# Two-layer GLA/NSA trunk with mixture of experts on one core: float32 diagonal products in the attention, three experts kept on chip for the combination, a tail that works on pairs of tiles, a branch hint for the TensorE

## The chip, the core and the metric

The kernel runs on one NeuronCore of one Trainium2 chip. Five engines work side by side, each with its own instruction stream in fixed order: PE (TensorE, matrix products), DVE (VectorE), ACT (ScalarE), POOL (GpSimd) and SP (SyncE, which here only issues DMAs). The metric is the device time of the core in microseconds (us), the median of several executions. The profile comes from one further execution, whose own time stands beside its span below.

## The reference, cut to what matters

The input x is 512 tokens by 1024 features in float32. Layer 0 is gated linear attention, layer 1 is native sparse attention (NSA), and each is followed by a mixture of 16 experts of which every token uses two. After each of the four parts the residual is added and a layer norm is taken.

```
for i in range(DEPTH):                       # 2 layers: GLA, then NSA
    h = mixer(x)
    x = layer_norm(DN_ALPHA * x + h, ln_g[i, 0], ln_b[i, 0])
    f = moe_ffn(x, ...)                      # 16 experts, top 2, SwiGLU
    x = layer_norm(DN_ALPHA * x + f, ln_g[i, 1], ln_b[i, 1])
```

In moe_ffn an expert computes silu(x Wg) * (x Wu), times the gate weight of the token, and then the down product with Wd; a token's result is the sum over its two experts. In NSA the selected-block and the window branch each are a masked softmax over causal keys followed by a product with the values V; with 512 tokens, 8 blocks of 64 and a window of 512 both cover all causal keys.

## The kernel before, in words

Tokens lie in four tiles t = 0..3 of 128. To keep float32 accuracy with fast products, most operands are split in two float16 parts (hi and lo), and a product is three float16 products: hi*hi, hi*lo, lo*hi. ACT makes hi, DVE or POOL makes lo as the difference.

**Experts (moe, L810 to L962).** Each expert takes up to CAP = 96 tokens. `collect` (L839) gathers the token rows of expert e by one-hot matrices `ohe` on PE, `hot` (L828) makes those matrices on POOL. The gate/up products stand in L910 to L912, the hidden part `hh` is evacuated by ACT and DVE, and the down product is L944 to L946. While expert e is computed, `dispatch(e + 2)` collects the one after next, and `take` splits weights on ACT (L179) and DVE (L181). Weights come by SP's DMAs into seven staging buffers. The result rows `y` of experts 0 to 13 go to a DRAM table `yslots` (L955), and when expert 13's rows have landed, POOL issues eight indirect DMAs (L959) that add the two rows of each token to x: the order of (choice c, tile t) is (0,0), (0,1), (1,0), (0,2), (1,1), (0,3), (1,2), (1,3), and the second of a tile waits for its first. The last KEEP = 2 experts stay on chip: their rows are kept as float16 pairs `yh` (L949, L950), and `add_last` (L352) multiplies them by transposed one-hot matrices `ohT` on PE (L359) and adds the result to x, either on DVE (L369) or by an ACT copy (L366) and a POOL add (L367).

**A branch.** `dense_moe` (L964) handles an expert with more than 96 tokens. Every engine loads the largest load `rt_ci` (L966) and branches (L967). For these inputs the branch body, some 865 instructions of PE, is jumped over in both layers. The branch stands in expert 0: in layer 0 PE meets it in the middle of its gate/up product, in layer 1 at the end of it.

**Attention of layer 1 (nsa_attn, L1375).** It handles units (t, g, b): token tile t, key group g, branch b. The eight units of t = 3 come first, then t = 2, 1, 0. A unit makes score tiles for key tiles j = t..0 (L1418, L1419), ACT takes exp into `pf` (L1421), POOL masks the diagonal tile j = t (L1424), and `split` makes hi (ACT L1386, L1388 or DVE L1390 by the table HI_BY) and lo (DVE L1394; off the diagonal two of three on POOL, L1392, by LO_BY). `pv` multiplies by V: three float16 products per head and key tile (L1435 to L1437). Scores run two units ahead. Output projections and norms of finished tiles are placed between the units (ATTN_FILL).

**Tail (finish_out, L320).** After layer 1's experts the sums of all four tiles are formed by add_last (OUT_ADD says which halves go by ACT and POOL), and tiles (0,1) and then (2,3) are normed: statistics, a chain of one-column operations for the inverse root of each tile (ln_scale, L307), two 512-wide passes for each half tile, on DVE or (four of eight) on ACT and POOL, and the store.

The instruction order is the scheduler's, close to the order of the code.

Of the kernel before, what the change touches and what calls it, by code (L numbers as in the profile page):

```python
# [9 lines left out]
F32 = mybir.dt.float32  # L10
F16 = mybir.dt.float16
BF16 = mybir.dt.bfloat16
I32 = mybir.dt.int32
# [20 lines left out]
LO_BY = 'pdp'  # L34
OUT_ADD = (0, 0), (1, 0), (1, 1), (1, 1)
OUT_DVE = 1, 5, 6, 7
OUT_DIR = -1
PRELUDE = ("r0 r1 o0 t2 r2 oa s2 ob rt rs c0 t3 s3 r3 c1 xb",
# [16 lines left out]
RINGS = "aaallll" * 3 + "aaalllll" * 3 + "aaa", "aaallll" * 7  # L55
KEEP = 2
HS = 16.0
NEG = -1e30


class Trunk:
# [258 lines left out]
    def finish_out(self, store):  # L320
        nc = self.nc
        V = nc.vector
        lng, lnb = self.moe_ln
        scales, after = {}, None
        for t in range(NT):
            self.add_last(t, OUT_ADD[t])
        for pair in ((0, 1), (2, 3)):
            for t in pair:
                for n in range(2):
                    with self.behind(after):  # L330
                        last = V.bn_stats(self.bns[t][:, n], self.x[t][:, n * 512:n * 512 + 512])
            for t in pair:
                with self.behind(last):
                    self.bn = self.bns[t]
                    _, mean, z, b = self.ln_scale()
                    after = V.scalar_tensor_tensor(b, mean, -1.0, z, op0=OP.mult, op1=OP.mult)
                scales[t] = mean, z, b
            for t in pair[::OUT_DIR]:
                mean, z, b = scales[t]
                for h in range(2):  # L340
                    hs = slice(h * 512, h * 512 + 512)
                    s, g, o = self.x[t][:, hs], lng[:, hs], lnb[:, hs]
                    if 2 * t + h in OUT_DVE:
                        V.scalar_tensor_tensor(s, s, mean, g, op0=OP.subtract, op1=OP.mult)
                        V.scalar_tensor_tensor(s, s, z, o, op0=OP.mult, op1=OP.add)
                    else:
                        nc.scalar.activation(s, s, AF.Identity, bias=b, scale=z)
                        nc.gpsimd.tensor_mul(s, s, g)  # L348
                        nc.gpsimd.tensor_add(s, s, o)  # L349
                    store(t, h)  # L350

    def add_last(self, t, pool=()):  # L352
# [457 lines left out]
    def moe(self, layer, xT, ahead=()):  # L810
# [89 lines left out]
        first = []  # L900
        for e in range(NE):
            wg, wu, wd = self.W[e]
            xh, oh = XH.pop(e)
# [18 lines left out]
            hh = self.tmp([P, 2, 2, CAP], F16, "hh", 2)  # L922
            h3 = h.rearrange("p (f c) -> p f c", f=2)
            hh_ins = self.hilo(hh[:, 0], hh[:, 1], h3)
            nc.scalar.activation(g[:CAP, 1:3], o, AF.Copy, scale=IWS / HS, accum_out=gs)
            if e == 0:
                self.dense_moe(layer, xT, gm, ci)
            if e + 2 >= AHEAD:
                dispatch(e + 2)
            self.take(2, () if e else (sg_ins,))  # L930
            self.take(1, () if e else (sg_ins,))
            if e == NE - 2:
                first = [self.load_unit(src, slot="l") for src in ahead]
                self.ring = False
            if e >= NE - KEEP:
# [20 lines left out]
            if e == NE - KEEP - 1:  # L956
                for c, t in ((0, 0), (0, 1), (1, 0), (0, 2), (1, 1), (0, 3), (1, 2), (1, 3)):
                    j = c * NT + t
                    nc.gpsimd.indirect_dma_start(  # L959
                        out=self.x[t], out_offset=None, in_=self.yslots[:],  # L960
                        in_offset=bass.IndirectOffsetOnAxis(ap=gi[:, j:j + 1], axis=0), compute_op=OP.add)
        return first  # L962

    def dense_moe(self, layer, xT, gm, ci):  # L964
        nc, tc, a = self.nc, self.tc, self.a
        load = nc.values_load(ci[0:1, 0:1], min_val=0, max_val=2 * S)  # L966
        with tc.If(load > CAP, preferred_fallthrough_block=False):  # L967
            dm = self.tmp([P, NT, NE], F32, "rt_dm", 1)
# [104 lines left out]
    def nsa_proj(self, first, PT):  # L1073
# [9 lines left out]
        kB = [PT([P, 4, S], f"kB{b}") for b in range(2)]  # L1083
        V = [[PT([P, 4, 129], f"V{b}{t}") for t in range(NT)] for b in range(2)]
        qA = [PT([P, NT, 4, P], f"qA{g}") for g in range(4)]
        qB = [PT([P, NT, S], f"qB{g}") for g in range(4)]
# [285 lines left out]
        rest = lambda: v1(0), lambda: v1(1), lambda: cv(0), lambda: cv(1)  # L1372
        return (kcA, kcB, vc, kA, kB, V, qA, qB, gate), rest

    def nsa_attn(self, T, pool, early, rest, kcA, kcB, vc, kA, kB, V, qA, qB, gate):  # L1375
        nc = self.nc
# [3 lines left out]

        def split(hi, lo, src, ps=None):
            i = cnt[0]
# [6 lines left out]
            else:  # L1389
                nc.vector.tensor_copy(hi, src)  # L1390
            if ps is not None and LO_BY[i % len(LO_BY)] == "p":
# [21 lines left out]
        def scores(t, g, b):  # L1413
            ph = self.wp.tile([P, 4, 2, S], F16, name="ph", tag="wst", bufs=NST)
            for j in range(t, -1, -1):
# [3 lines left out]
                nc.tensor.matmul(st, kB[b][:70, g, js], qb(g, t), start=False, stop=True)  # L1419
                pf = T([P, S], "pf", F32, 3)  # L1420
                self.exp_ins = nc.scalar.activation(pf, st, AF.Exp)  # L1421
                if j == t:
                    v = pf.rearrange("p (h q) -> p h q", h=4)
                    nc.gpsimd.affine_select(v, v, pattern=[[0, 4], [1, P]], compare_op=OP.is_ge, fill=0.0,  # L1424
                                            base=0, channel_multiplier=-1)
                split(ph[:, j, 0], ph[:, j, 1], pf, None if j == t else st)
            return ph

        def pv(t, g, b, ph):
            ob = self.bank()  # L1430
            for h in range(4):
                hs = slice(h * P, (h + 1) * P)
                o0 = ob[:, h * 65:(h + 1) * 65]
                for j in range(t + 1):
                    nc.tensor.matmul(o0, ph[:, j, 0, hs], V[b][j][:, g, 0:65], start=(j == 0), stop=False)  # L1435
                    nc.tensor.matmul(o0[:, :64], ph[:, j, 0, hs], V[b][j][:, g, 65:129], start=False, stop=False)
                    nc.tensor.matmul(o0, ph[:, j, 1, hs], V[b][j][:, g, 0:65], start=False, stop=(j == t))  # L1437
            return ob
# [206 lines left out]
```

## Time and profile before

| what | value |
|---|---|
| median of 3 runs | 992.65 us (988.48 to 994.8) |
| the profiled execution's own time | 996.98 us |
| its span (first to last instruction) | 995.3 us |
| PE busy | 868.1 us (87%) |
| DVE busy | 767.5 us (77%) |
| ACT busy | 571.5 us (57%) |
| POOL busy | 353.4 us (36%) |
| mean granted TensorE clock | 0.94 |

The span divides into stages with different limits: layer 0's attention to about 240 us, its experts to 411, the NSA projections to about 587, the attention units to 746, routing to about 795, layer 1's experts to 957, and the tail. A row of a timeline gives start, duration, engine, line, operation, result and operands, and in brackets how long the engine was idle before it and what ended the wait; "issue" is a wait for nothing that the profile shows.

### The profile page before, as it was taken

What the parts mean: (1) busy time and instruction counts of PE and PEld (TensorE: products, weight loads), DVE (VectorE), ACT (ScalarE), POOL (GpSimd) and SP (SyncE); (2) the same over time, 40 slices, a digit from 0 to 9 for tenths busy, and PEclk for the clock granted to TensorE, in tenths of its full rate; (3) what the DMA queues carried; (4) which work ended last, traced back from release to release, by engine and by line L of the source; (5) the groups of instructions that cost most, each with busy time, mean ns of one, the idle gap of its engine ahead of it and who ended that gap; (6) DMA issues with size and microseconds to landing.
All of it is one profiled execution on the core that took longest, in us unless ns stands there. A gap on an engine that the chain in (4) does not pass through costs nothing. (4 is left out here: it accounts for less than half of the span.)

```text
span 995.3 us, 26759 instructions
## 1 busy us (share of the span) xinstructions
PE 868.1 (87%) x11266; PEld 708.6 (71%) x11266; DVE 767.5 (77%) x1675; ACT 571.5 (57%) x1196; POOL 353.4 (36%) x375
## 2 busy tenths in 40 slices
PE   7999999995799999699989989787987569999960
PEld 2478888875788888488978868465766558988840
DVE  5962226989699998797697756898798969999738
ACT  4832432542499999515535347765447149999821
POOL 0210120023135330540384425686532319523056
PEclk9999999997799999999999999788999679999995
DMA  9652231253499995942330010300018349999282
GB/s 299 222 207 86 85 114 57 86 213 127 142 385 394 368 380 213 213 143 83 128 127 3 2 43 2 129 2 1 2 47 336 128 149 409 380 380 379 100 154 100
DMA packets 29393, 169.64 MB, mean 170 GB/s; under 512 B 3536, under 2 KB 4176, under 8 KB 12752
## 3 DMA queue, kind: packets, MB, share of 16 engines
q1 hardware_dynamic: 23168, 144.49, 38.7%
q0 software_dynamic: 2960, 12.32, 5.7%
q10 hardware_dynamic: 3136, 11.01, 3.0%
q8 instruction: 93, 1.52, 0.6%
q14 instruction: 36, 0.29, 0.1%
HBM read 153.91 MB, written 13.89 MB: 169 GB/s over the span
## 5 line engine op out<-in xcount | busy, mean ns | idle before, releaser
L828 POOL TENSOR_SCALAR ohe<-icap,rt_px 128x96 f16<-128x96 f32 x112 | 111.6, 1011 | 153.2 <-PE bank L915 144.5
L181 DVE SCALAR_TENSOR_TENSOR whl<-wsu,whl 128x512 f16<-128x512 f32 x192 | 127.3, 713 | 3.0 <-ACT whl L179 2.2
L181 DVE SCALAR_TENSOR_TENSOR whl<-wst,whl 128x512 f16<-128x512 f32 x116 | 75.5, 702 | 67.3 <-ACT whl L179 67.2
L839 PE MATMUL bank<-ohe,xs 128*128 128x96 f16 x2048 | 103.7, 215 | 15.6 <-issue 8.6
L839 PEld LDWEIGHTS <-xs 128*128 128x128 f16 x2048 | 98.7, 104 | 16.6 <-issue 12.1
L179 ACT ACTIVATE whl<-wsu 128x512 f16<-128x512 f32 x192 | 106.8, 624 | 3.3 <-PE bank L259 3.2
L179 ACT ACTIVATE whl<-wst 128x512 f16<-128x512 f32 x144 | 80.8, 624 | 29.9 <-PE bank L250 9.8
L181 DVE SCALAR_TENSOR_TENSOR wha<-wst,wha 128x512 f16<-128x512 f32 x144 | 93.9, 703 | 1.7 <-ACT wha L179 1.7
L257 PE MATMUL bank<-whl,xt 128*128 128x256 f16 x320 | 88.1, 275 | 0.8 <-ACT xt L232 0.7
L259 PE MATMUL bank<-whl,xt 128*128 128x256 f16 x320 | 87.4, 274 | 1.4 <-DVE xt L233 1.4
L258 PE MATMUL bank<-whl,xt 128*128 128x256 f16 x320 | 88.1, 275 | 0.0
L179 ACT ACTIVATE wha<-wst 128x512 f16<-128x512 f32 x144 | 79.7, 622 | 2.5 <-DMA wst<-moe 2.5
L910 PE MATMUL bank<-xh,whl 128*128 128x96 f16 x576 | 75.2, 206 | 0.0
L911 PE MATMUL bank<-xh,whl 128*128 128x96 f16 x576 | 75.2, 206 | 0.0
L912 PE MATMUL bank<-xh,whl 128*128 128x96 f16 x576 | 75.2, 206 | 0.0
L259 PE MATMUL bank<-whl,oT 128*128 128x256 f16 x256 | 70.6, 276 | 2.2 <-DVE oT L233 2.2
L257 PE MATMUL bank<-whl,oT 128*128 128x256 f16 x256 | 70.7, 277 | 0.8 <-ACT oT L232 0.5
L258 PE MATMUL bank<-whl,oT 128*128 128x256 f16 x256 | 70.6, 276 | 0.0
L258 PE MATMUL bank<-whl,xT 128*128 128x256 f16 x256 | 69.8, 273 | 0.0
L259 PE MATMUL bank<-whl,xT 128*128 128x256 f16 x256 | 69.8, 273 | 0.0
L257 PE MATMUL bank<-whl,xT 128*128 128x256 f16 x256 | 69.8, 273 | 0.0
L911 PE MATMUL bank<-xh,wha 128*128 128x96 f16 x448 | 62.7, 212 | 4.3 <-issue 4.3
(388 smaller groups left out, 2813.2 us busy)
## 6 DMA issues: line engine op xcount, KB each, us to landing
wsu<-moe SPq DMA_DIRECT2D x54, 1024.0 KB, 7.8
wst<-moe SPq DMA_DIRECT2D x42, 1024.0 KB, 7.9
wst<-gla_in SPq DMA_DIRECT2D x11, 1024.0 KB, 4.8
yslots<-y ACTq DMA_DIRECT2D x28, 384.0 KB, 6.9
wst<-nsa_in SPq DMA_DIRECT2D x9, 1024.0 KB, 4.8
wst<-gla_out SPq DMA_DIRECT2D x4, 1024.0 KB, 4.8
wha<-nsa_out SPq DMA_DIRECT2D x4, 1024.0 KB, 4.9
xs<-xT SPq DMA_DIRECT2D x4, 512.0 KB, 7.1
```

The lines of the kernel that those rows point to most:

```text
L179: self.hi_ins = nc.scalar.activation(hl[:, 0, s], st[:, s], AF.Copy, scale=WS)
L181: nc.vector.scalar_tensor_tensor(hl[:, 1, s], st[:, s], WS, hl[:, 0, s], op0=OP.mult, op1=OP.subtract)
L257: nc.tensor.matmul(out, xt[0][:, k], w[0][:, s], start=(k == 0), stop=False)
L258: nc.tensor.matmul(out, xt[0][:, k], w[1][:, s], start=False, stop=False)
L259: nc.tensor.matmul(out, xt[1][:, k], w[0][:, s], start=False, stop=(k == KT - 1))
L828: eng.tensor_scalar(part[e][0][:, t], self.icap, self.px[:, t, e:e + 1], None, op0=OP.is_equal)
L839: nc.tensor.matmul(banks[half][:, j * CAP:(j + 1) * CAP], xs[t][:, i, k * P:(k + 1) * P], oh[:, t], start=(j == 0 and t == self.order[0] a ...
L910: nc.tensor.matmul(o, w[0][:, s], xh[:, 0, k], start=(k == 0), stop=False)
L911: nc.tensor.matmul(o, w[1][:, s], xh[:, 0, k], start=False, stop=False)
L912: nc.tensor.matmul(o, w[0][:, s], xh[:, 1, k], start=False, stop=(k == KT - 1))
```

## The change

It has five parts. (1) Attention: for t = 0, 1, 2 the diagonal tile j = t is no longer split; exp writes it as float32, and PE multiplies it with a float32 copy `VF` of V in one float32 product per head. Six `VF` tiles are made by ACT when V is evacuated. For these t POOL makes no lo parts any more (`share` only for t = 3). (2) KEEP is 3: expert 13 stays on chip too, so the gathers follow expert 12, and the combination takes six products for each half tile instead of four. (3) Gate/up of expert 15 comes before the down product of 14. (4) The branch body follows the branch directly, and PE gets a prefetch hint that the branch is likely taken; one hint for each layer. (5) Tail: tiles 0 and 1 are summed on DVE; for tiles 2 and 3 PE adds x itself, by a float32 product with the identity, so that their statistics and their first pass read PSUM; the small operations run for two tiles at once on two columns; three half tiles go over ACT and POOL.

```diff
-KEEP = 2
+KEEP = 3
+HINT = mybir.BranchHintType.__args__[0]
@@ finish_out
-        for t in range(NT):
-            self.add_last(t, OUT_ADD[t])
+        for t in (0, 1):
+            self.add_last(t)
+            src[t] = [self.x[t][:, h * 512:h * 512 + 512] for h in range(2)]
+        for t in (2, 3):
+            src[t] = self.sum_last(t)
...
+            st = self.tmp([P, 6, 2], F32, "lnp", 2)
...
+            for c in (3.0, 12.0, 768.0):
+                V.tensor_mul(u, z, z)
+                V.tensor_mul(u, u, v)
+                V.scalar_tensor_tensor(z, u, c, z, op0=OP.subtract, op1=OP.mult)
+            after = V.scalar_tensor_tensor(b, mean, -1.0, z, op0=OP.mult, op1=OP.mult)
...
+    def sum_last(self, t):
...
+            self.nc.tensor.matmul(ps, self.identf, self.x[t][:, ns], start=True, stop=False)
+            for e in range(KEEP):
+                for i in range(2):
+                    self.nc.tensor.matmul(ps, self.ohT[:CAP, e, t * P:(t + 1) * P], self.yh[e][:CAP, i, ns],
+                                          start=False, stop=(e == KEEP - 1 and i == 1))
@@ moe
+        self.tc.mark_branch_hint_location(f"dense{layer}", HINT, [mybir.EngineType.PE])
...
+        for e in range(NE):
+            sg_ins = up(e)
+            if e == 0:
+                self.dense_moe(layer, xT, gm, ci)
+            if e + 2 >= AHEAD:
+                dispatch(e + 2)
+            self.take(3, () if e else (sg_ins,))
+            if e == NE - 2:
+                first = [self.load_unit(src, slot="l") for src in ahead]
+                self.ring = False
+                continue
+            if e == NE - 1:
+                down(NE - 2)
+            down(e)
@@ dense_moe
-        with tc.If(load > CAP, preferred_fallthrough_block=False):
+        with tc.If(load > CAP, label=f"dense{layer}"):
@@ evac_v
+                    if tp * 2 + j < NT - 1:
+                        vf = VF[b][tp * 2 + j]
+                        nc.scalar.activation(vf[:, :, 0:64], ps[:, j], AF.Copy, scale=IWS)
+                        nc.gpsimd.memset(vf[:, :, 64:65], 1.0)
@@ scores
-                pf = T([P, S], "pf", F32, 3)
+                exact = j == t < NT - 1
+                pf = ph[:, j].rearrange("p i q -> p (i q)").bitcast(F32) if exact else T([P, S], "pf", F32, 3)
...
-                split(ph[:, j, 0], ph[:, j, 1], pf, None if j == t else st)
+                if not exact:
+                    split(ph[:, j, 0], ph[:, j, 1], pf, None if j == t else st, t == NT - 1)
@@ pv
+                if exact:
+                    pf = ph[:, t].rearrange("p i q -> p (i q)").bitcast(F32)
+                    nc.tensor.matmul(o0, pf[:, hs], VF[b][t][:, g], start=True, stop=(t == 0))
```

Where the rows of an engine move, three places matter. The first is PE at the branch of layer 0 (`rt_ci` is the load, `dw` the branch body's weights, `wha` the gate/up weights of expert 0). Before:

```order
L910 MATMUL bank<-xh,wha 128x96
L966 TENSOR_LOAD rt_ci
L967 COMPARE_AND_BRANCH
L967 UNCONDITIONAL_BRANCH
L970 COMPARE_AND_BRANCH
```

Of the change, the first rows of PE's program, the branch, and what stands behind its body:

```order
L1689 UNCONDITIONAL_BRANCH
L1689 BRANCH_PREFETCH_HINT
L482 LDWEIGHTS wl
...
L1002 TENSOR_LOAD rt_ci
L1003 COMPARE_AND_BRANCH
L1006 COMPARE_AND_BRANCH
...
L1003 UNCONDITIONAL_BRANCH
L1689 BRANCH_PREFETCH_HINT
L936 LDWEIGHTS wha
```

The hint for layer 0 is PE's first instruction, the one for layer 1 stands directly behind layer 0's body, and the unconditional branch has moved from the head of the body to its end.

The second place is ACT at the end of layer 1's experts (`sg` evacuates the gate/up product, `hh` the hidden part, `y` and `yh` the down product; the rows begin with expert 13's down product). Before:

```order
L953 ACTIVATE y<-bank,gslot 96x512 x2
L955 DMA yslots<-y 96x1024
L919 ACTIVATE sg<-bank 128x192
L232 ACTIVATE hh<-h 128x192
L925 ACTIVATE gslot<-bank 96x2
L949 ACTIVATE yh<-bank,gslot 96x512 x2
...
L949 ACTIVATE yh<-bank,gslot 96x512 x2
L366 COPY more<-bank 128x512 x5
```

Of the change:

```order
L970 ACTIVATE yh<-bank,gslot 96x512 x2
L944 ACTIVATE sg<-bank 128x192
L231 ACTIVATE hh<-h 128x192
L949 ACTIVATE gslot<-bank 96x2
L944 ACTIVATE sg<-bank 128x192
L231 ACTIVATE hh<-h 128x192
L949 ACTIVATE gslot<-bank 96x2
L970 ACTIVATE yh<-bank,gslot 96x512 x4
L353 ACTIVATE r_12389<-r_12389,lnp 128x512
```

Expert 13's table write is gone, both gate/up evacuations stand ahead of the last four down evacuations, and the five copies for POOL's adds are gone. Layer 0 ends in the same way, with weight splits of the next layer in between.

The third place is DVE in the tail, from the statistics of tiles 2 and 3 on (`lnst` and `lnp` hold the small columns). Before, the statistics read x, and each small operation stands once for each tile:

```order
L331 BN_STATS bn<-r_11697 128x6 x2
L331 BN_STATS bn<-r_11043 128x6 x2
L311 BN_AGGR lnst<-bn 128x2 x2
L312 TENSOR_SCALAR lnst<-lnst 128x1
```

Of the change, three of the four statistics stand ahead of everything, they read PSUM, and the small operations have two columns:

```order
L335 BN_STATS bn<-bank 128x6 x3
L337 BN_AGGR lnp<-bn 128x2
L357 SCALAR_TENSOR_TENSOR r_11613<-bank,lnp,lng 128x512
L335 BN_STATS bn<-bank 128x6
L337 BN_AGGR lnp<-bn 128x2
L339 TENSOR_SCALAR lnp<-lnp 128x2
```

For a pair of tiles 13 small operations follow instead of 20.

## Rows read from the trace of the kernel before

**Rows 1.** Page, DMA queues: PE's instruction queue (packets, MB, share).

```profile
q8 instruction: 93, 1.52, 0.6%
```

**Rows 2.** Branch line L967: PE's branches, ns min/median/max.

```profile
L967 PEldq COMPARE_BRANCH x4: 81/2054/5040, 251.2 to 799.2; - x4
```

**Rows 3.** Timeline behind the two branches: start, us, engine, line [idle before].

```profile
255.74 0.26 PE L911 MATMUL bank<-xh,wha 128*128 128x96 f16 x1 [4.26 <-issue]
...
799.10 3.54 POOL L828 TENSOR_SCALAR ohe<-icap,rt_px 128x96 f16<-128x96 f32 x4 [7.72 <-PEq L967]
...
804.29 1.46 PE L839 MATMUL bank<-ohe,xs 128*128 128x96 f16 x16 [5.29 <-issue]
808.88 3.38 PE L839 MATMUL bank<-ohe,xs 128*128 128x96 f16 x40 [3.13 <-issue]
...
810.43 0.49 ACT L232 ACTIVATE xh<-bank 128x384 f16<-128x384 f32 x1 [8.93 <-issue]
```

**Rows 4.** Windows: us, PE, PEld, DVE, ACT, POOL busy; PEclk, DMA, GB/s.

```profile
795.00:800.00 5.00, 4.00 (x79) 3.91 (x76) 4.16 (x12) 0.90 (x3) 0.90 (x2) 0.86 0.04 7
```

**Rows 5.** Timeline, end of layer 0's experts and first sum.

```profile
383.57 0.31 ACTq L955 DMA_DIRECT2D yslots<-y  x1
...
398.78 1.72 POOL L959 DMA_INDIRECT r<-yslots,rt_gi  x1 [27.04 <-DVE whl L181]
...
408.33 0.42 PE L944 MATMUL bank<-wha,hh 128*96 128x512 f16 x1 [1.21 <-ACT hh L232]
...
415.81 1.29 DVE L369 TENSOR_TENSOR r<-r,bank 128x512 f32<-128x512 f32 x2 [3.18 <-DMA r<-yslots,rt_gi]
```

**Rows 6.** Windows of the attention units of t = 2, 1, 0 (columns as rows 4).

```profile
632.50:682.50 50.00, 39.77 (x511) 28.38 (x508) 46.48 (x94) 30.79 (x58) 36.43 (x33) 0.83 0.06 23
682.50:715.00 32.50, 27.68 (x359) 20.88 (x356) 25.02 (x58) 15.75 (x30) 17.59 (x20) 0.89 0.00 1
715.00:746.50 31.50, 25.73 (x369) 19.03 (x366) 30.16 (x94) 16.24 (x29) 14.07 (x16) 0.92 0.11 38
```

**Rows 7.** Lines in 632.5 to 746.5: lo parts; count | busy, mean ns.

```profile
L1394 DVE TENSOR_TENSOR ph<-pf,ph 128x512 f16<-128x512 f32 x26 | 24.1, 935 | 0.3 <-ACT ph L1386 0.3
...
L1392 POOL TENSOR_TENSOR ph<-pf,ph 128x512 f16<-128x512 f32 x22 | 31.3, 1427 | 4.7 <-ACT ph L1386 2.7 <-DVE ph L1390 1.3 <-DVE lnst L317 0.4
```

**Rows 8.** PE: a float32 product by form; first and last of 48 float16.

```profile
L544 PE MATMUL bank<-qd,kd 128*128 128x128 f32 x32 | 4.2, 275 | 0.0
...
596.42 0.19 PE L1435 MATMUL bank<-V,ph 128*128 128x65 f16 x1
...
597.86 0.19 PE L1437 MATMUL bank<-V,ph 128*128 128x65 f16 x1
```

**Rows 9.** Timeline: layer 1's table writes and gathers, and what waits for them.

```profile
931.81 0.31 ACTq L955 DMA_DIRECT2D yslots<-y  x1
...
941.59 0.31 ACTq L955 DMA_DIRECT2D yslots<-y  x1
...
945.36 1.73 POOL L959 DMA_INDIRECT r<-yslots,rt_gi  x1 [26.28 <-DMA yslots<-y]
...
973.38 2.48 POOL L367 TENSOR_TENSOR r<-r,more 128x512 f32<-128x512 f32 x2 [1.10 <-DMA r<-yslots,rt_gi]
```

**Rows 10.** Timeline, PE: down product 14 and the one-hot combination.

```profile
946.27 0.42 PE L944 MATMUL bank<-wha,hh 128*96 128x512 f16 x1 [1.21 <-ACT hh L232]
...
957.30 7.07 PE L359 MATMUL bank<-yh,ohT 96*128 96x512 f16 x32
```

**Rows 11.** Tail on DVE and POOL: timeline; of tile lnst, ns min/median/max.

```profile
961.88 1.28 DVE L369 TENSOR_TENSOR r<-r,bank 128x512 f32<-128x512 f32 x2 [2.91 <-PE bank L359]
...
990.74 1.59 POOL L349 TENSOR_TENSOR r<-r,lnb 128x512 f32<-128x512 f32 x1
...
L316 DVE TENSOR_SCALAR lnst<-lnst x12: 257/265/274, 973.1 to 987.6; 128x1 f32<-128x1 f32 x12
...
L345 DVE SCALAR_TENSOR_TENSOR r<-r,lnst,lnb x4: 742/745/1751, 976.7 to 989.5; 128x512 f32<-128x512 f32 x4
```

More of the change, by code (lines that the diff above doesn't have):

```diff
@@ L323, in finish_out @@
         lng, lnb = self.moe_ln
-        scales, after = {}, None
-        for t in range(NT):
-            self.add_last(t, OUT_ADD[t])
+        src = {}
+        for t in (0, 1):
[3 more added lines that the diff above has]
+            src[t] = self.sum_last(t)
+        after = None
         for pair in ((0, 1), (2, 3)):
-            for t in pair:
-                for n in range(2):
+            st = self.tmp([P, 6, 2], F32, "lnp", 2)
+            for i, t in enumerate(pair):
+                for h in range(2):
@@ L330, in finish_out @@
                     with self.behind(after):
[L331 to L345, printed above, removed]
-                    else:
-                        nc.scalar.activation(s, s, AF.Identity, bias=b, scale=z)
-                        nc.gpsimd.tensor_mul(s, s, g)
-                        nc.gpsimd.tensor_add(s, s, o)
+                        V.bn_stats(self.bns[t][:, h], src[t][h])
@@ new lines, in finish_out @@
+                with self.behind(after):
+                    V.bn_aggr(st[:, 0:2, i], self.bns[t].rearrange("p a b -> p (a b)"))
+            mean, var, v, u, z, b = (st[:, i] for i in range(6))
+            V.tensor_scalar(v, var, 2.0 ** 26, EPS / (ALPHA * ALPHA) * 2.0 ** 26, op0=OP.mult, op1=OP.add)
+            V.tensor_scalar(u.bitcast(I32), v.bitcast(I32), 1, None, op0=OP.logical_shift_right)
+            V.tensor_scalar(z.bitcast(I32), u.bitcast(I32), -1.0, float(0x5F3759DF) - 2.0 ** 31, op0=OP.mult, op1=OP.add)
@@ L898, in moe, with up @@
         gi, gh, gm, ci = self.route()
+        self.tc.mark_branch_hint_location(f"dense{layer}", HINT, [mybir.EngineType.PE])
         self.take(6 - self.taken, (self.gated,))
-        first = []
-        for e in range(NE):
-            wg, wu, wd = self.W[e]
+        first, part_e = [], {}
+        def up(e):
+            wg, wu, _ = self.W[e]
             xh, oh = XH.pop(e)
@@ L922, in moe, with down @@
             hh = self.tmp([P, 2, 2, CAP], F16, "hh", 2)
-            h3 = h.rearrange("p (f c) -> p f c", f=2)
-            hh_ins = self.hilo(hh[:, 0], hh[:, 1], h3)
+            self.hilo(hh[:, 0], hh[:, 1], h.rearrange("p (f c) -> p f c", f=2))
             nc.scalar.activation(g[:CAP, 1:3], o, AF.Copy, scale=IWS / HS, accum_out=gs)
[L926 to L934, printed above, removed]
+            part_e[e] = hh, gs
+            return sg_ins
+        def down(e):
+            wd = self.W[e][2]
+            hh, gs = part_e.pop(e)
             if e >= NE - KEEP:
@@ L1084, in nsa_proj @@
         V = [[PT([P, 4, 129], f"V{b}{t}") for t in range(NT)] for b in range(2)]
+        VF = [[PT([P, 4, 65], f"VF{b}{t}", F32) for t in range(NT - 1)] for b in range(2)]
         qA = [PT([P, NT, 4, P], f"qA{g}") for g in range(4)]
@@ L1372, in nsa_proj, with nsa_attn @@
         rest = lambda: v1(0), lambda: v1(1), lambda: cv(0), lambda: cv(1)
-        return (kcA, kcB, vc, kA, kB, V, qA, qB, gate), rest
-    def nsa_attn(self, T, pool, early, rest, kcA, kcB, vc, kA, kB, V, qA, qB, gate):
+        return (kcA, kcB, vc, kA, kB, V, VF, qA, qB, gate), rest
+    def nsa_attn(self, T, pool, early, rest, kcA, kcB, vc, kA, kB, V, VF, qA, qB, gate):
         nc = self.nc
```

34 lines of the change are left out of this document (26 added, 8 removed).

## The prediction

> **What bounds the kernel now.** I read the windows by stage first, then the timeline of the engine that is late in each stage, because the limits change along the span. In the steady part of both expert stages PE works without gaps, so what the change does there counts only at the ends. I therefore looked at four places where PE or DVE stands still.
>
> The first is the jump over the branch body. PE's branch instruction takes up to 5.04 us where its smallest takes 0.08 [rows 2]. Behind it PE idles 4.26 us in layer 0; in layer 1 it idles 5.29 us, does 16 products, and idles 3.13 us more, with nothing that the profile shows to wait for [rows 3]. The second is the end of layer 0's experts: DVE waits 3.18 us for a gather before it can form tile 0's sum [rows 5]. The third is the attention for t = 2, 1, 0: DVE is busy 46.5 of 50 us, 25.0 of 32.5 and 30.2 of 31.5 [rows 6], so it sets the pace at t = 2 and t = 0, and neither engine alone at t = 1. The fourth is the tail: the down product of expert 15 is followed by the combination at 957.3 [rows 10], DVE forms the first sum at 961.9, the last gathered tile is there at 973.4 [rows 9], POOL ends at 992.3 [rows 11], and the span, 995.3, closes 3.0 us later.
>
> **The branch hint.** PE's instructions come by a queue of their own in 93 packets of 1.52 MB, some 16 KB each [rows 1]. The two stalls are such fetches, if what follows the jump was not on hand. If the hint brings the target early, layer 0 gains its 4.2 us: the rest of expert 0's gate/up product needs nothing new. In layer 1 the next limit is POOL, whose four one-hot matrices are ready at 799.10 + 3.54 = 802.6. The first half collection is 32 products: 1.46 us for 16 [rows 3], some 2.6 for all, so ACT can start at 805.2 instead of 810.43, a gain of 5.2. ACT idled 8.9 us for it, and the DMAs move 7 GB/s just before [rows 4], because all staging is full; so the splits and loads behind it move up with it. Together 9.4 us. Bounds: 0 if the hint does nothing; 10.6 if those 32 products run at the higher clock level, in about half of 2.6 us.
> [...]
>
> **KEEP = 3 and the order of 14 and 15, at the end of layer 0.** In layer 1 POOL's first gather starts 945.36 - 941.59 = 3.8 us after the issue of the table write that it waits for [rows 9]. Expert 12's write in layer 0 is issued at 383.57, so the first gather moves from 398.78 to about 387.4 [rows 5], 11 us earlier, and the 3.18 us wait goes. What is late next is expert 15's `yh`. PE waited 1.21 us for `hh` ahead of expert 15's down product [rows 5] and as long or more ahead of 14's; with both gate/up products first, each wait lies under the other's work. So down 15, which started at 408.33 and takes 12 products of 0.22 [rows 10], ends at 408.5 instead of 411; two evacuations (1.4 together) and two products later tile 0 can be summed, at about 410.8 instead of 415.81: 5.0. PE then has 16 more one-hot products (3.5 us) before it can turn tile 0; DVE's norm of 6 us covers most of it, and I take 4.5. Bounds: 1 (gathers slowed by the weight loads of the next layer that they now meet) and 5.0.
>
> **Attention.** In the stretch of t = 2, 1, 0 there are 26 lo parts on DVE (mean 935 ns) and 22 on POOL (1427 ns) [rows 7]: 48 tiles. After the change only the 24 off the diagonal remain, all on DVE. So DVE's own count hardly falls; what goes is 31 us of POOL work on two SBUF operands, beside which DVE is slow: passes of the same 128x512 size range from 742 to 1751 ns in the tail [rows 11]. Taking 0.74 for a lo part without POOL beside it, 24 cost 17.8 instead of 24.1; the rest of DVE's 101.7 us [rows 6] shrinks less, since POOL keeps its masks and adds: I take 8 us, 14 in all. ACT loses some 20 copies and no longer waits for POOL's mask before each.
> Against this PE pays. The 48 float16 products from 596.42 to 597.86 come every 0.031 us, three for 0.092 [rows 8]. A float32 product shows as two records: 16 products of 128 columns make 32 records in 4.2 us, 0.131 each [rows 8], so 0.26 for one. With 65 columns it is between 0.13 (by columns) and 0.26 (by the weight load); the operands that are swapped for every head make it the latter, so 0.26. That is 0.17 more for each of 96, 5.4 us for each t. At t = 2 PE has 10.2 us idle [rows 6]: gain 4. At t = 1 it has 4.8 idle: no gain. At t = 0 DVE loses some 9 us and PE has 5.8 idle, of which part is used: gain 3. Sum 7. Bounds: 14 gained (DVE's saving whole), 16 lost (all PE cost on the path).
> [...]
>
> **Tail.** Expert 12's write is issued at 931.81, expert 13's at 941.59 [rows 9], so all gathers move 9.8 us, the last landing from 973.4 to 963.6. Without the waits ahead of the down products (1.21 and one more like it [rows 10]) down 15 ends at 954.9, and its `yh` is ready at 956.3. PE's 24 products for tiles 0 and 1 (0.22 each, four of them done before) end at 960.3; tiles 2 and 3 take four times 1.3 plus a float32 identity product of 512 columns (two records, four times the columns of 128, 1.0), 9.3 us, ending at 969.6 as the gathers allow. DVE: sums and statistics of tile 1 at 961.7 (0.64 a pass [rows 11]), 13 small operations of 0.2 to 0.27 us [rows 11] and two first passes 4.6, two second passes 1.5: 967.8. Statistics of tiles 2 and 3, 2.6, to 970.4; small ones and three first passes 5.3, three second passes 2.2 to 3.5 (POOL beside them): 978 to 979. POOL's one half of the last pair ends with it, at 979.3, and 3.0 us later the span closes: 982.3 instead of 995.3, a gain of 13. Bounds: 8 (all passes slowed to 1.6 by POOL) and 15.
>
> **Small costs.** Six VF evacuations and four more transposes in each layer lie beside work of other engines; I count 0.6 in all.
>
> **The sum.** 9.4 + 4.5 + 7 + 13 - 0.6 = 33.3. The profiled execution took 996.98, so 963.7; it lies 4.3 above the median of the runs, 992.65, so about 959 on their scale. From here all times are on that scale.
>
> **The rivals.**
> The hint changes nothing. For it: the body still lies between branch and target, and the hint for layer 0 is armed thousands of instructions ahead. Against: it names this branch and this engine, and only PE's stalls are long. 959 + 9.4, about 968. Chance 0.18.
> PE becomes the attention's bound. For it: PE is busy 25.7 of 31.5 and 27.7 of 32.5 us at t = 0 and 1, at granted clocks of 0.92 and 0.89 [rows 6], and gets 5.4 more in each. Against: busy times overlap short gaps, and ACT's waits for POOL go. With all 16 us on the path instead of 7 gained: 982. Chance 0.12.
> The gathers do not come earlier by as much, because each tile's second waits for its first and they now meet other DMAs. If tile 3 still lands at 973.4, two identity products and six one-hot products a half (4.6), statistics, small ones, passes and close (13) give 991, a tail gain of 4 to 5; 968. Chance 0.09.
> [...] Chance 0.03.
>
> **How the numbers follow.** My forecast holds 0.56; 0.02 is left for mixtures. Its own range is 950 to 969 (tail 8 to 15, layer 0 end 1 to 5, attention 0 to 12 gained). The range for 8 in 10 takes in the rivals at 968 and part of the attention's: 944 to 977. Measured changes under about 1% (9.9 us) cannot be told from none here. Faster by more: the forecast, the hint's and the gathers' rivals whole, and 0.06 of the attention's: 0.90. Within 1%: 0.06. Slower: 0.04.
>
> **What would show it.** PE's branch rows under 0.1 us and no idle time over 1 us behind them would show the hint. The first gather at some 11 us earlier against expert 15's gate/up, and DVE's first sum ended by PE instead of a DMA, would show KEEP. The lo parts near 0.75 us, and PE's idle time in the three attention windows, tell whether DVE or PE bounds there. In the tail, statistics that wait for PE's identity products, and a last store some 22 us after the last `yh`, would show the rest. It would be wrong if the float32 products cost above 0.3 us each, or if the last gather lands as late as now.

## The result, and the profile after

The changed kernel takes 959.03 us, the median of 4 runs (957.8 to 959.84); the kernel before, run beside it, 991.13 us (988.48 to 994.8). The ratio is 0.967, with a 95% interval of 0.964 to 0.971. The predicted time was 959.0, and the time lies in the range. The profiled execution took 958.76 us, beside 996.98 before.

The total came out as predicted, its terms did not. To see where the time went I take one instruction that stands in both traces at the end of each stage and subtract its two starts. The lead of the changed kernel is then:

| stage (instruction compared) | before, us | after, us | lead | of it in this stage | predicted |
|---|---|---|---|---|---|
| up to the first branch (routing) | 242.67 | 243.00 | -0.3 | -0.3 | 0 |
| branch of layer 0 (expert 2's `h`) | 282.00 | 275.30 | 6.7 | 7.0 | 4.2 |
| end of layer 0 (copy into `kB`) | 460.89 | 454.82 | 6.1 | -0.6 | 4.5 |
| NSA projections, t = 3 (scores of t = 2) | 626.46 | 622.13 | 4.3 | -1.8 | -0.6 |
| attention t = 2, 1, 0 (last reciprocal) | 746.55 | 730.45 | 16.1 | 11.8 | 7 |
| output projection, routing (first `xh`) | 793.31 | 776.84 | 16.5 | 0.4 | 0 |
| branch of layer 1 (`h`) | 849.46 | 823.33 | 26.1 | 9.6 | 5.2 |
| experts of layer 1 (`xh`) | 936.98 | 911.58 | 25.4 | -0.7 | 0 |
| tail (end of the span) | 995.3 | 956.7 | 38.6 | 13.2 | 13 |

These 38.6 us are more than the 32.1 between the medians, since the profiled execution of before was a long one (996.98). Rows of less than some 1.3 us cannot be told from nothing: a second trace of the changed kernel differs from the first by up to that much in one stage (e12 below). The page of the changed kernel, its span, engines and granted clock in 40 slices:

```profile
span 956.7 us, 26589 instructions
PE 879.4 (92%) x11218; PEld 722.4 (76%) x11218; DVE 743.5 (78%) x1662; ACT 557.6 (58%) x1178; POOL 313.9 (33%) x353
PEclk9999999998899999989999999979999879999997
```

PE now works 92% of the span, POOL a third.

**The branches.** PE's branch rows of the changed kernel (ns min/median/max) answer to [rows 2]:

```profile
L1003 PEldq COMPARE_BRANCH  x2: 365/638/912, 251.6 to 782.0; - x2
```

There are two instead of four, and the longest takes 0.91 us instead of 5.04. The timeline behind them answers to [rows 3]:

```profile
252.78 0.21 PE L936 MATMUL bank<-xh,wha 128*128 128x96 f16 x1 [0.94 <-PEq L1003]
...
782.54 3.58 POOL L851 TENSOR_SCALAR ohe<-icap,rt_px 128x96 f16<-128x96 f32 x4 [7.63 <-PEq L1003]
782.59 2.88 PE L862 MATMUL bank<-ohe,xs 128*128 128x96 f16 x64
784.78 0.48 ACT L231 ACTIVATE xh<-bank 128x384 f16<-128x384 f32 x1
```

PE idles 0.94 us in layer 0 (4.26 before); in layer 1 its collection starts at 782.59 with no wait, where it had waited 5.29 and 3.13 us. The products do not wait for POOL's four one-hot matrices either: PE is through its 64 by 785.5, POOL with the matrices at 786.1. The clock shows a second gain. Windows of before (columns as in [rows 4]), then of after:

```profile
256.00:261.00 5.00, 3.50 (x46) 3.29 (x44) 1.47 (x3) 1.99 (x5) 1.93 (x3) 0.50 0.59 213
805.00:810.00 5.00, 1.87 (x25) 1.66 (x23) 0.00 (x0) 0.00 (x0) 0.00 (x0) 0.50 0.29 120
810.00:815.00 5.00, 5.00 (x46) 3.97 (x44) 3.56 (x7) 3.98 (x11) 0.00 (x0) 0.66 0.00 2
```

```profile
256.00:261.00 5.00, 5.00 (x74) 3.86 (x71) 4.65 (x10) 4.91 (x13) 2.14 (x3) 1.00 0.76 241
783.00:788.00 5.00, 4.38 (x68) 3.46 (x65) 5.00 (x11) 5.00 (x13) 3.11 (x4) 1.00 0.91 308
```

Before, PE came out of each stall at a granted clock of 0.50; after, it stays at 1.00.

**The end of layer 0.** Timeline of the changed kernel, answering to [rows 5]:

```profile
383.39 1.73 POOL L980 DMA_INDIRECT r<-yslots,rt_gi  x1 [19.68 <-DVE whl L180]
...
405.67 0.67 DVE L392 TENSOR_TENSOR r<-r,bank 128x512 f32<-128x512 f32 x1
...
408.53 1.54 POOL L980 DMA_INDIRECT r<-yslots,rt_gi  x1 [6.82 <-DMA r<-yslots,rt_gi]
...
417.33 2.48 POOL L390 TENSOR_TENSOR r<-r,more 128x512 f32<-128x512 f32 x2
419.85 1.07 ACT L389 COPY more<-bank 128x512 f32<-128x512 f32 x2 [8.08 <-POOL r L390]
420.81 1.10 ACT L231 ACTIVATE xt<-bank 128x512 f16<-128x512 f32 x2
421.48 0.40 PE L256 MATMUL bank<-whl,xt 128*128 128x256 f16 x1 [6.87 <-ACT xt L231]
```

The first gather comes 15.4 us earlier than the 398.78 of before, 8.5 beyond the lead of 6.9; tile 0's sum comes 10.1 us earlier (415.81 before), 3.3 beyond the lead, with no wait for a gather. Then a new wait eats it: ACT stands 8.08 us before it may copy tile 3's sum, until POOL has added tile 2's copies; the split of tile 0 stands behind that copy on ACT; and PE idles 6.87 us for the split.

**Attention.** Windows of t = 2, 1, 0, the stages of [rows 6] moved by the lead:

```profile
628.20:674.30 46.10, 44.16 (x491) 34.67 (x488) 42.47 (x105) 28.70 (x55) 16.69 (x19) 0.85 0.07 24
674.30:703.20 28.90, 28.65 (x336) 23.87 (x333) 18.35 (x55) 11.35 (x22) 9.38 (x13) 1.00 0.01 1
703.20:730.40 27.20, 26.95 (x303) 22.59 (x302) 21.12 (x79) 11.17 (x20) 8.65 (x13) 1.00 0.05 14
```

PE is busy all but 0.25 us of each of the last two, at a granted clock of 1.00; DVE has 20 us less, POOL half of what it had. Of the lines of 628.2 to 730.4, the lo parts (answering to [rows 7]) and the float32 product; then a timeline row of eight such products (16 records) in a row:

```profile
L1480 PE MATMUL bank<-VF,ph 128*128 128x65 f32 x192 | 34.9, 294 | 0.0
...
L1435 DVE TENSOR_TENSOR ph<-pf,ph 128x512 f16<-128x512 f32 x24 | 18.4, 777 | 0.2 <-ACT ph L1427 0.2
```

```profile
728.41 2.00 PE L1480 MATMUL bank<-VF,ph 128*128 128x65 f32 x16
```

A lo part on DVE takes 0.78 us (0.94 before), and a float32 product 2.00 / 8 = 0.25 us at a granted clock of 1.00.

**Tail.** First the issue of the last gather before, then the timeline of the changed kernel, answering to [rows 9] and [rows 11]:

```profile
967.00 1.54 POOL L959 DMA_INDIRECT r<-yslots,rt_gi  x1 [5.91 <-DMA r<-yslots,rt_gi]
```

```profile
910.26 1.72 POOL L980 DMA_INDIRECT r<-yslots,rt_gi  x1 [16.81 <-DVE whl L180]
...
930.54 0.67 DVE L392 TENSOR_TENSOR r<-r,bank 128x512 f32<-128x512 f32 x1
930.58 1.54 POOL L980 DMA_INDIRECT r<-yslots,rt_gi  x1 [4.70 <-DMA r<-yslots,rt_gi]
...
941.00 1.89 DVE L335 BATCH_NORM_STATS2 bn<-bank 128x6 f32<-128x512 f32 x3
...
948.74 3.08 DVE L358 SCALAR_TENSOR_TENSOR r<-r,lnp,lnb 128x512 f32<-128x512 f32 x3
...
951.35 1.59 POOL L355 TENSOR_TENSOR r<-r,lnb 128x512 f32<-128x512 f32 x1
```

From the first sum to the end of the span 26.2 us pass, 33.4 before, and DVE waits for no gather in between. Nor does it wait for PE: the statistics of tiles 2 and 3 start at 941.00 without a wait.

### The profile page after: what moved, and what is told of

Same layout as the page of the kernel before. It is cut to its first block, busy times and chain, and to the rows that moved or that the text cites. A ratio compares the mean times of both kernels' runs of the same rounds, so it can differ in the third digit from the quotient of the medians.

```text
span 956.7 us, 26589 instructions
## 1 busy us (share of the span) xinstructions
PE 879.4 (92%) x11218; PEld 722.4 (76%) x11218; DVE 743.5 (78%) x1662; ACT 557.6 (58%) x1178; POOL 313.9 (33%) x353
## 5 line engine op out<-in xcount | busy, mean ns | idle before, releaser
L862 PE MATMUL bank<-ohe,xs 128*128 128x96 f16 x2048 | 99.4, 212 | 6.7 <-DVE ohe L851 5.5
L862 PEld LDWEIGHTS <-xs 128*128 128x128 f16 x2048 | 94.9, 101 | 7.3 <-DVE ohe L851 4.5
L258 PE MATMUL bank<-whl,oT 128*128 128x256 f16 x256 | 69.6, 273 | 1.6 <-DVE oT L232 1.6
L256 PE MATMUL bank<-whl,oT 128*128 128x256 f16 x256 | 69.7, 273 | 0.5 <-ACT oT L231 0.5
L257 PE MATMUL bank<-whl,oT 128*128 128x256 f16 x256 | 69.7, 273 | 0.0
```

The lines of the kernel that those rows point to most:

```text
L256: nc.tensor.matmul(out, xt[0][:, k], w[0][:, s], start=(k == 0), stop=False)
L257: nc.tensor.matmul(out, xt[0][:, k], w[1][:, s], start=False, stop=False)
L258: nc.tensor.matmul(out, xt[1][:, k], w[0][:, s], start=False, stop=(k == KT - 1))
L862: nc.tensor.matmul(banks[half][:, j * CAP:(j + 1) * CAP], xs[t][:, i, k * P:(k + 1) * P], oh[:, t], start=(j == 0 and t == self.order[0] a ...
```

## The experiments

All start from the changed kernel (959.0) unless said otherwise. Times are medians of 4 to 6 runs.

**The changed kernel again (e12).** 

> The changed kernel itself once more, since the other runs were compared with its 959.0 from another time, and the kernel before was found anywhere from 988 to 998. If the comparison holds: 957 to 961, all executions within 3 us, while the kernel before spreads over 6 to 10 us again. If the level of the chip moves by more than that from time to time: outside, and differences under some 5 us in the runs above say nothing.

Measured: 960.01 us (958.03 to 961.16), beside 988.0 to 998.4 for the kernel before. So the level holds to 1 us, and the wide spread belongs to the kernel before. By stage the two traces of the changed kernel differ by 1.3 us up to the first branch (244.34 against 243.00), 1.1 in the projections, and less elsewhere.

**Without the hint (e1).**

```diff
-        self.tc.mark_branch_hint_location(f"dense{layer}", HINT, [mybir.EngineType.PE])
```

> The changed kernel (959.0) without the call that places the branch hint; the label stays. The prediction's step (the hint gives back the two waits for the target alone, 9.4): 968.4. Theory from the two traces (the wait also leaves TensorE at its low clock level and holds up the products behind it, 7.1 in layer 0 and 9.2 in layer 1): 975, with PE's branch rows at 4 to 5 us again and a granted clock of 0.5 behind each. Rival (the stalls came and went by themselves): 959.

Measured: 968.42 us (964.9 to 969.9), 9.4 more. PE's branch row, and the windows behind the two branches:

```profile
L1002 PEldq COMPARE_BRANCH  x2: 3672/3706/3739, 253.0 to 788.6; - x2
```

```profile
256.00:262.00 6.00, 5.12 (x66) 5.16 (x67) 1.96 (x4) 1.89 (x5) 1.82 (x3) 0.50 0.46 180
...
792.00:798.00 6.00, 5.53 (x66) 5.33 (x67) 3.47 (x7) 2.14 (x7) 1.98 (x3) 0.50 0.87 336
```

Both branches take 3.7 us again, and the clock is 0.50 behind both. In this trace the two places cost 4.5 and 2.9 us, not the 7.0 and 9.6 of the comparison above: the kernel before loses more at its branches than the changed kernel does without the hint.

**Without the hint, old form of the If (e5).** The hint line of e1 is gone, and:

```diff
-        with tc.If(load > CAP, label=f"dense{layer}"):
+        with tc.If(load > CAP, preferred_fallthrough_block=False):
```

> The changed kernel without the hint (968.4 in the run before) and with the old form of the If (preferred_fallthrough_block=False, no label). The prediction gave the form of the If nothing: then 968. Theory from the trace without the hint (there each layer shows one wait of 3.4 to 3.6 us and half as many branch rows, where the kernel before shows a second wait of 3.1 us after 16 products in layer 1): the old form costs a second wait for instructions, 3 to 6 us with the clock that falls with it, so 971 to 975.

Measured: 969.32 us (964.8 to 970.7). My theory was wrong: the old form costs nothing measurable. PE's row has four branches again, one long one in each layer, but there is one wait in each layer (3.88 and 4.24 us), not a second one:

```profile
L1002 PEldq COMPARE_BRANCH  x4: 81/1862/3992, 251.6 to 784.5; - x4
```

So the traces of the changed code show the second wait of 3.13 us in layer 1 [rows 3] neither with nor without the hint; that of e5 is of its fastest execution (964.84), and its slower ones, 968.4 to 970.7, have none. The wait goes with the kernel before as far as the traces show; which part of the change removed it, and why it stood there, no run tells.

**The kernel before with the hint alone (e10).** The hint line and the labelled If of the change, nothing else.

> The kernel before with one part of the change alone: the hint and the labelled If. Its own runs lie in two groups, 988 to 991 and 995 to 998. Theory (the waits for the branch target differ from run to run and make the two groups; the hint removes them): one group, within 3 us of each other, at 978 to 982. Rival (the groups come from elsewhere, and the hint is worth the 9.4 that it cost to take it out): two groups again, near 980 and 987.

Measured: 983.47 us (982.5 to 983.8; ratio 0.990, 0.986 to 0.993), beside 988.4 to 997.2 for the kernel before, median 994.35. The hint is worth 10.9 us alone (7 to 14 by the interval), about what it costs to take it out; and five executions lie within 1.3 us, where those of before spread over 9. PE's branch row, and the timeline in layer 1:

```profile
L969 PEldq COMPARE_BRANCH  x2: 532/618/703, 252.9 to 791.8; - x2
```

```profile
792.66 0.84 PE L840 MATMUL bank<-ohe,xs 128*128 128x96 f16 x16 [0.42 <-PEq L969]
795.63 3.44 PE L840 MATMUL bank<-ohe,xs 128*128 128x96 f16 x48 [2.13 <-issue]
```

The wait at the jump is gone (0.42 us); the second one, behind 16 products, is still there with 2.13. So the hint lifts the first, and something else in the change took the second away. Measured like the stages above, the two branches of this trace are 7.4 and 8.5 us shorter than before: the hint alone gives 15.9 of the 16.6 between the two profiles, and the second wait is worth the 1.2 us by which layer 1's branch is still longer than in the changed kernel. Why the same stall costs 15.9 us there and 7.4 in e1 is open; the profile of the kernel before is of one of its long executions.

**Float16 diagonals, lo parts shared again (e2).**

```diff
-                exact = j == t < NT - 1
+                exact = False
...
-                    split(ph[:, j, 0], ph[:, j, 1], pf, None if j == t else st, t == NT - 1)
+                    split(ph[:, j, 0], ph[:, j, 1], pf, None if j == t else st, True)
```

(and `exact = False` in `pv`.) 

> The changed kernel (959.0) with the attention's old diagonals: float16 pairs, lo parts shared between DVE and POOL again. The VF copies are still made, but not read. The prediction's step (7 gained): 966. Theory from the traces (12 gained, since PE no longer idles and so keeps its high clock level): 971, with PE idle some 20 us again in t = 2, 1, 0. Rival (the float32 products cost what they save): 959.

Measured: 973.78 us (972.8 to 974.6), 14.8 more, and PE is busy 93.1 of 114 us in the three stages, as in [rows 6]. By the medians the attention part was worth twice what I predicted. By stage, 11.8 of the 14.4 us by which this trace is longer lie in the attention units, as many as in the table above; the rest lies mostly ahead of them, in stages that the edit leaves alone.

**Float32 diagonals, lo parts shared again (e7).** Only the `True` of e2's diff.

> The changed kernel (959.0), float32 diagonals kept, but the lo parts off the diagonal shared between DVE and POOL as before. The prediction's reason (POOL's passes on two SBUF operands slow DVE, 0.94 instead of 0.74 us a lo part): most of the 14.8 us that the float16 diagonals cost come back, 968 or more, with lo parts on DVE above 0.9 us. Theory from the traces (what counted is that the diagonal's chain, ACT copy, mask on POOL, two splits, got shorter, and PE waits for it no more): 963 or less.

Measured: 972.43 us (969.5 to 973.8), 13.4 more. Lines of its stages, then windows and a timeline row:

```profile
L1433 POOL TENSOR_TENSOR ph<-pf,ph 128x512 f16<-128x512 f32 x15 | 19.4, 1293 | 7.6 <-ACT ph L1427 5.4 <-DVE ocf L1507 1.6 <-DVE ph L1431 0.5
...
L1435 DVE TENSOR_TENSOR ph<-pf,ph 128x512 f16<-128x512 f32 x9 | 9.8, 1089 | 0.0
```

```profile
676.00:688.00 12.00, 9.11 (x100) 6.66 (x97) 8.31 (x21) 4.56 (x10) 5.80 (x7) 0.78 0.01 1
688.00:700.00 12.00, 12.00 (x93) 9.59 (x94) 6.10 (x19) 4.21 (x7) 4.21 (x7) 0.65 0.00 0
```

```profile
681.01 0.18 PE L443 MATMUL bank<-wrs,xt 128*128 128x16 f16 x1 [2.64 <-DVE xt L232]
```

The prediction's reason held: with 15 lo parts on POOL, one on DVE takes 1.09 us instead of 0.78. But the waits themselves are small; PE is idle 6.4 of 111.5 us. The larger price, by the estimate that follows, is the clock. PE waits 2.64 us once for DVE, and over the 24 us that hold this wait and what comes behind it PE is granted 0.78 and 0.65: 9.11 x 0.22 + 12 x 0.35 = 6 us of work at a clock of 1.00 are lost by this estimate, of the 9 that this trace loses in the stages.

**Float16 diagonals, all lo parts on DVE (e9).** `exact = False` twice, the `share` argument left as in the change.

> The changed kernel (959.0) with float16 diagonals, but all lo parts of t = 2, 1, 0 on DVE, none on POOL. With e2 and e7 this completes the four combinations. If POOL's lo parts alone cost the time (with float32 diagonals they cost 13.4): 960 to 962. If both halves of the change are needed (DVE, busy 82 of 102 us after, gets 24 more lo parts at 0.78 and some casts, 20 to 25 us, and becomes the bound of these stages): 967 or more, with DVE busy nearly throughout and PE idle and at the low clock level in stretches.

Measured: 966.7 us (965.5 to 968.1), 7.7 more. Lines and windows:

```profile
L1435 DVE TENSOR_TENSOR ph<-pf,ph 128x512 f16<-128x512 f32 x48 | 35.4, 756 | 1.0 <-ACT ph L1429 0.6 <-ACT ph L1427 0.2
```

```profile
628.00:676.00 48.00, 40.28 (x504) 28.55 (x502) 42.89 (x108) 30.43 (x59) 16.84 (x18) 0.82 0.07 23
676.00:706.00 30.00, 26.05 (x361) 20.76 (x361) 25.73 (x61) 15.90 (x31) 12.77 (x14) 0.94 0.01 2
706.00:738.00 32.00, 26.38 (x384) 19.40 (x383) 30.86 (x99) 17.38 (x31) 10.97 (x14) 0.95 0.07 21
```

DVE is the bound at t = 0 (30.9 of 32), as expected. So of 14.8 us, taking the lo parts off POOL brings 7.1 by itself, float32 diagonals by themselves 1.4, and both 14.8. In the attention units of the traces it is 4.1, 2.8 and 11.8. Either way only both together leave PE nearly without gaps: 2.4 us idle of 102.2, against 20.9 of 114 (e2), 6.4 of 111.5 (e7) and 17.3 of 110 (e9).

**KEEP = 2 (e4).**

```diff
-KEEP = 3
+KEEP = 2
```

> The changed kernel (959.0) with KEEP = 2; the order of 14 and 15 and the new tail stay. The prediction's steps (gathers 9.8 earlier are worth most of 4.5 in layer 0 and of 13 at the end): 970 or more. Theory from the traces (layer 0 gained nothing from KEEP, since the third kept row takes one of five shared row buffers; at the end the gathers have about 5 us in hand): 960 to 964, with DVE's wait for a gather back at the end of layer 0, and ACT's wait of 8 us for POOL gone.

Measured: 964.96 us (964.6 to 967.0), 5.9 more. Timeline at the end of layer 0 and in the tail:

```profile
415.34 0.60 ACT L231 ACTIVATE xt<-bank 128x512 f16<-128x512 f32 x1 [7.56 <-PE bank L273]
...
932.49 1.28 DVE L392 TENSOR_TENSOR r<-r,bank 128x512 f32<-128x512 f32 x2 [5.09 <-DMA r<-yslots,rt_gi]
...
941.22 2.07 PE L367 MATMUL bank<-r,identf 128*128 128x512 f32 x2 [11.87 <-DMA r<-yslots,rt_gi]
```

It is two effects of opposite sign. At the end of layer 0 KEEP = 2 gains 3.3 us on the changed kernel (its lead over it goes from 0.8 to 4.1): the split of tile 0 waits for PE's transposes, not for POOL. In the tail it loses 9.9 (963.4 - 956.7 = 6.7 behind, from 3.2 ahead): DVE waits for gathers, and PE 11.87 us for one.

**Old tail (e3).** `finish_out` as before, KEEP = 3.

> The changed kernel (959.0) with finish_out as it was before (sums by add_last, small operations tile by tile), KEEP = 3 kept. If the rewritten tail carries the 13 us that the end gained: 972. If the earlier gathers carry them: before, 33.4 us pass from the first sum to the end, of which the wait for the last gather is part; after, 26.2; so at most 7.2 are the rewriting's, and 962 to 966 is expected.

Measured: 963.23 us (961.9 to 963.7), 4.2 more. So the rewriting carries 4.2 of the tail's 13, the earlier gathers the larger part (9.9 in e4's trace).

**Old order of 14 and 15 (e8).**

```diff
-                continue
-            if e == NE - 1:
-                down(NE - 2)
             down(e)
```

> The changed kernel (959.0) with the down product of 14 in front of the gate/up of 15 again, KEEP = 3 kept. The prediction's step (each wait for hh lies under the other product): the waits of 1.2 to 1.7 us ahead of both down products come back; in layer 1 they are on the path, so 961 to 962. Rival (the wait only moves on, to the yh that the combination needs): 959 to 960.

Measured: 960.96 us (960.0 to 963.6), 1 to 2 more than the changed kernel's 959.0 and 960.0. PE's timeline in layer 1:

```profile
919.90 0.42 PE L965 MATMUL bank<-wha,hh 128*96 128x512 f16 x1 [1.21 <-ACT hh L231]
...
928.12 0.42 PE L965 MATMUL bank<-whl,hh 128*96 128x512 f16 x1 [1.21 <-ACT hh L231]
```

The two waits are back as predicted, 2.4 us, and from the last `xh` to the end this trace takes 2.8 us more; by the medians the difference is at the edge of what can be told.

**Tile 3 added by DVE at the end of layer 0 (e6), then tiles 2 and 3 (e11).** In `nsa_proj`; `late` collects the adds that `add_last` would have made. The diff is that of e11; in e6 tile 2 keeps its line and its copies, and the block with `add2` is absent.

```diff
-        self.add_last(2, (1, 1))
-        self.add_last(3, (1, 1))
+        add2, add3 = [], []
+        self.add_last(2, late=add2)
+        self.add_last(3, late=add3)
         with self.behind(last):
             xt[0] = self.transpose_split(self.x[0], "xt0")
+        with self.behind(self.split_ins):
+            for f in add2:
+                last = f()
+        with self.behind(last):
             last = self.moe_norm(1)
+        with self.behind(last):
+            for f in add3:
+                f()
```

> The changed kernel (959.0) in which, at the end of layer 0, tile 3 is no longer copied by ACT and added by POOL, but added by DVE straight from PSUM, behind the split of tile 0. Theory (the third kept row takes one of five shared row buffers, so ACT's copy for tile 3 waits for POOL, and tile 0's split stands behind it on ACT): PE starts its projections at about 416 instead of 421.5, and the time is 954. Rival (PE would wait there anyway, for the gathers or the weights): 959.

Measured: 956.39 us (954.2 to 958.2), 2.6 less, half of what I expected. The trace is of the slowest execution (958.2) and is only 0.8 us shorter at the end of layer 0; where the rest lies is not shown. ACT and PE:

```profile
419.44 1.08 ACT L231 ACTIVATE xt<-bank 128x512 f16<-128x512 f32 x2 [6.79 <-POOL r L390]
...
420.09 0.28 PE L256 MATMUL bank<-whl,xt 128*128 128x256 f16 x1 [4.60 <-ACT xt L231]
```

With tile 3's copy gone, the split itself waits for POOL: it needs the row buffer of tile 2's copy. 

> The changed kernel (959.0) in which, at the end of layer 0, neither tile 2 nor tile 3 is copied to a row buffer for POOL: DVE adds both straight from PSUM, tile 2 right behind the split of tile 0. Theory (with one of the two copies gone, tile 0's split still waited 6.8 us for POOL's add, since it needed the buffer of the other; with both gone it has none to wait for): PE starts its projections at about 416 instead of 421.5, and the time is 954 to 956. Rival (the adds of tiles 2 and 3, now on DVE behind their gathers, hold up tile 1's norm as much): 958 to 960.

Measured: 953.71 us (950.1 to 956.8; ratio to before 0.960, 0.956 to 0.963), 5.3 less than the changed kernel. The same rows:

```profile
416.42 1.09 ACT L231 ACTIVATE xt<-bank 128x512 f16<-128x512 f32 x2 [10.44 <-PE bank L273]
...
417.07 0.28 PE L256 MATMUL bank<-whl,xt 128*128 128x256 f16 x1 [0.25 <-ACT xt L231]
```

The split waits for PE's transposes alone, and PE starts 4.4 us earlier (1.2 of them its lead from the stages ahead) and idles 0.25 us. That settles what the split waited for, and this version beats both kernels. By stage it gains 2.9 us at the end of layer 0, of the 4.8 by which its trace is shorter; the rest is spread over other stages in steps of up to 1 us.

## Why the prediction was right, and where not

The sum, 33.3, stood against 32.1 between the medians. Two of its terms were off by 5 us each, the end of layer 0 and the attention, and they offset each other; a third, the hint, fits the medians but not the two traces. That the total fits so well is in part luck.

**The hint** (9.4): right in size on the medians, 9.4 out of the changed kernel and 10.9 into the one before. Of what the runs changed, the hint alone lifts the stall at the jump: with it the longest branch takes 0.7 to 0.9 us (e10, the changed kernel), without it 3.7 (e1), 4.0 (e5) and 5.0 (before). That the stalls are fetches of instructions, and that the queue of [rows 1] is PE's, was the author's estimate: the queue holds 1.52 of the 1.81 MB (84%) of the page's two instruction queues, and PE and PEld have 84% of the instructions in the span; no view shows a fetch beside a stall. Two steps failed inside the term. "Branch rows under 0.1 us" did not come. And I made POOL's four one-hot matrices the next limit in layer 1; after, PE's collection runs ahead of them, so they belong to later products. I also left out what the clock adds: in the windows above, of before and of e1, a stall is followed by 5 us and more at a granted clock of 0.50. Between the two profiled executions the branches gave 16.6. By e10's trace nearly all of it, 15.9, is the hint's, with the clock that follows each stall; by e1's trace the hint is worth 7.4, by the medians 9.4 and 10.9. The long profiled execution of before is part of that difference; the rest is open.

**The end of layer 0** (4.5, bounds 1 to 5.0): wrong, it gave -0.6, outside its bounds. The gathers came earlier and tile 0 was summed earlier, but by less than I had. Set back by the lead, the first gather gained 8.5 us instead of 11.4, and the sum 3.3 instead of 5.0, with ACT's last `yh` behind four splits of the next layer's weights (400.62 to 402.8). The step that failed most is the one from tile 0's sum to PE's first projection. DVE's norm did cover the 16 more products, which end at 413.6 with the norm at 413.3; but behind the sum I followed only PE and DVE. The third kept row is one of five buffers that `yh`, `more`, `ohT` and `xt` share, so the copies of tiles 2 and 3 could no longer stand beside it, and ACT, in order, waited for POOL with tile 0's split behind. e4 and e11 show it: a row fewer, or no copies, and the wait is gone, and the stage gains 3.3 and 2.9 us. Without it the stage would have given some 2 us, inside my bounds but under 4.5. Part of what e11 lacks is the clock: PE waits 2.24 us for ACT's `yh` there, is granted 0.50 behind it, and its next 16 one-hot products take 0.43 us each instead of 0.22, so that it turns tile 0 at 415.77, 2.0 us after the norm. In the changed kernel, behind a wait of 1.62 us at the same place, PE was still granted 1.00.

**Attention** (7): the direction and the two prices were right. A lo part fell to 0.78 (I took 0.74), a float32 product costs 0.25 (0.26). Its weight loads took 0.20 us in the mean (L1480 PEld), those of the float16 products of before 0.11 (L1437 PEld); whether they or the columns set its price is not shown. The step that failed is the one from prices to gain: at t = 1 I set PE's 5.4 us of extra work against 4.8 of idle time and got no gain; 3.6 came. I held the clock at its 0.89. With DVE no longer late, PE idled 0.25 us in each of t = 1 and 0, and was granted 1.00 there. PE's busy time, 27.7 before, is 28.65 after, not 33. So the rival "PE becomes the attention's bound" came true in form, 99.8 of 102.2 us, and wrong in price. By the medians e2 puts the part at 14.8, just beyond my upper bound of 14; by its trace 11.8, inside it.

**The tail** (13): right, by its steps. Set back by the lead of 25.4, I had expert 15's `yh` at 930.9, the last statistics at 945, DVE's end at 952.6 to 953.6 and the span's at 956.9; measured were 930.6, 944.4, 951.8 and 956.7. The rival "the gathers do not come earlier" fell: the last is issued at 930.58, 11 us earlier than the 967.00 of before less the lead. One sign that I named did not come: no statistics wait for PE's identity products, since DVE is busy without a gap. e8 confirms the waits ahead of the down products, e3 and e4 split the term into 4.2 for the rewriting and the larger rest for the gathers.

**The projections** (-0.6): -1.8. Of it 1.6 falls at one place: PE waits 3.1 us for the same `QT` in both traces, and in the trace of after the granted clock fell behind it, to 0.66 over 5 us. My term was for the VF copies, and no run shows them: e10, which has none, loses 2.7 us in this stage, with the same 3.1 us wait and a granted clock of 0.66 over the 5 us behind it, as in the changed kernel. Windows of before, then of after:

```profile
500.00:512.00 12.00, 8.77 (x127) 7.58 (x125) 11.70 (x24) 5.67 (x13) 11.72 (x14) 1.00 0.25 89
```

```profile
494.00:507.50 13.50, 10.26 (x126) 8.76 (x124) 11.85 (x23) 5.58 (x13) 11.58 (x13) 0.87 0.30 107
```

## What to carry over

Price an idle stretch of PE with the clock that follows it, and work added to PE with the idle time it fills: here PE was granted 0.50 behind the stalls of before and of e1, and the two stages in which it hardly waited (0.25 us each) were granted 1.00, where it had been 0.89 and 0.92, and ended sooner with more work in them. When a value is kept longer, count every tile that shares its buffers, and look at which in-order engine stands behind the one that now waits. A total that fits says little about its terms; compare the lead stage by stage, and trace the same kernel twice to see how far a stage varies by itself.

## What was not expected of the hardware

The kernel before varies by 9 to 10 us from one execution to the next (988.0 to 998.4); with the hint alone five executions lie within 1.3 us, and the changed kernel without it spreads over 5 to 6 again (e1, e5). The longest branch without the hint took 3.7, 4.0 and 5.0 us in three traces (e1, e5, before). That its length also changes from one execution of a kernel to the next, and makes the spread, is not shown: each was traced once, and e11 spreads over 6.7 us with the hint. And behind a wait of 3.1 us the granted clock was lower in one execution (0.87, the changed kernel) and not in another (1.00, before), worth some 1.5 us, so that a difference of 2 us between two single profiles proves nothing.
